# A four-layer fp32 trunk: where ScalarE and VectorE make the parts of the first FFN's down weights

## The chip, the cores and the metric

The kernel runs on one core of one Trainium2 chip. The metric is device time in microseconds (us) of one execution of the whole program. TensorE (PE) multiplies matrices into PSUM banks, ScalarE (ACT) and VectorE (DVE) work element by element, GpSimd (POOL) does some small work and issues loads that add to what is there, and SyncE (SP) issues most of the loads from HBM. Each engine works through its own queue in order; semaphores tie the queues together.

## The reference

The program is a trunk of four layers on one sequence of 512 tokens and 1024 channels, all in fp32. Each layer is a mixer and an FFN with a norm ahead of each; the mixers are a diagonal state-space scan (S5) in layers 0 and 3, gated linear attention (GLA) in layer 1, and differential attention in layer 2. The change is in the first FFN, which computes

```
def rmsnorm(x, g):
    y = xf * lax.rsqrt(jnp.mean(xf * xf, axis=-1, keepdims=True) + NORM_EPS)
    return (y * g)

def swiglu_ffn(h, w_gate_up, w_down):
    g, u = jnp.split(h @ w_gate_up, 2, axis=-1)
    return (jax.nn.silu(g) * u) @ w_down

x = x + swiglu_ffn(rmsnorm(x, norm_ffn[layer]), ffn_w_gate_up[layer], ffn_w_down[layer])
```

with a hidden width of 2816, so `w_down` is 2816 x 1024.

## The kernel before

**Parts.** TensorE works on fp32r operands. To keep fp32 accuracy, each operand is split in two parts: the high part is a cast on ScalarE (`high`, line 348), the low part is the fp32 value minus the high part, on VectorE (`low`, line 356). Three matmuls (`mm3`, lines 376 to 378) then stand for one product: high by high, high by low, low by high.

**Weight tiles.** A weight tile of 128 x 1024 values (512 KB) is loaded by SP into one of three staging buffers (`wst`, line 337, `staged`), cast into one of five part buffers (`whl`), and subtracted. A staging buffer is free for the next load when its subtraction has been done; a part buffer when the last matmul on it is done. For the down weights, one such tile is a pair of k tiles (2 x 128 rows) by 512 output columns (`wb`).

**The FFN.** The hidden width is cut into 11 blocks of 256. For each block the gate and up columns come from seven products of quarter size instead of eight (`seven_block`; `seven_product`, line 543); its named steps run in a fixed order for the first two blocks and in program order for the rest. The last step of a block is `four` and `four_out`: VectorE scales the gate by the row norms (`scaled`, line 588, tile `g`), ScalarE applies silu (line 589), VectorE multiplies it by the other half (line 670), and ScalarE and VectorE make the activation's two parts (lines 680 and 681, tile `act`). In the first FFN (l = 0) the blocks are taken in groups of 3, 3, 3 and 2. After each group comes its down product (`gemm_b`): for each half `d` of the 1024 output columns, over the group's pairs of k tiles `kb`, two k tiles `a`, and four row tiles `t`, one `mm3` into one of four accumulators (`acc`). When the last k tile of an accumulator is done, VectorE adds it to x (line 526). The four accumulator banks are the ones that the gate products `a` and `c` use as well.

**Jobs.** The first and second FFN carry other work with them: after each `mm3`, `gemm_b` calls `self.job()`, which traces the next piece of a generator. In the first FFN this is `s5_spilled`, which prepares the matrices of the last layer's scan in eight rounds and spills them to HBM: small VectorE products (lines 1052 to 1054), ScalarE copies (lines 1119, 1142, 1262), small matmuls (`cps` line 1098, `xps` line 1200, `rps` line 1154) through two shared PSUM banks, and loads and stores on POOL. A job is tied behind the last high part, low part, gate scaling, silu and matmul that were traced before it:

```
    def job(self):
        with ExitStack() as c:
            for y in self.last.values():
                c.enter_context(self.tc.issue_after(y.ins))
            return next(self.jobs, None)
```

**What sets the order.** In this part the order in each engine's queue is made by the planner of the language from priorities and its own estimate of times; `issue_after(ins)` adds an edge by which the instructions traced under it stand behind `ins` in the queue of that engine. `self.last` keeps the latest `scaled` (gate scaling on VectorE) and `silu` (ScalarE). When `self.behind` is set, `high` is tied behind that silu and `low` behind that scaling. `gemm_b` sets `self.behind` from its argument in each step of `kb`, after the first pair's parts have been made, and with jobs it makes the parts of the next pair one step ahead (`nxt`). In the kernel before, the argument is given for the first column half in the FFNs 1 to 3 and is None in FFN 0.

Of the kernel before, what the change touches and what calls it, by code (L numbers as in the profile page):

```python
# [152 lines left out]
class Sides(Left):  # L153
# [19 lines left out]
    def ahead(self, n):  # L173

        w = [self.tr.staged(self.quarter(0, 0, b), 4, 256) for b in range(len(self.heads), len(self.heads) + n)]
        self.heads += [self.tr.halves(y, 4, 256) for y in w]
# [92 lines left out]
class Trunk:  # L269
# [107 lines left out]
        mm(out, lh, rl, start=False, stop=False)  # L377
        self.last["mm"] = mm(out, ll, rh, start=False, stop=last)  # L378

    def gemm_b(self, stat, w, nk, c0, evac, k0=0, tail=0, between=(), ahead=None, jobs=False, behind=None):  # L380

        between = iter(between)
        accs = [self.acc() for _ in range(NT)]
        hl = nxt = None
        for kb in range(0, nk - tail, 2):
            hl = nxt or self.wb(w, k0 + kb, c0)
            self.behind = behind
            nxt = self.wb(w, k0 + kb + 2, c0) if jobs and kb + 2 < nk - tail else None  # L390
            if kb == 2:
                self.flush()
            for a in range(2):
                k = kb + a
                for t in range(NT):
                    self.mm3(
                        accs[t][:], stat(k, 0, t), stat(k, 1, t), hl[:, 0, a], hl[:, 1, a],
                        k == 0, k == nk - 1,
                    )
                    if k == nk - 1:  # L400
                        evac(t, accs[t])
                    if jobs:
                        self.job()
            next(between, lambda: None)()
        self.behind = None
        if tail:
            hls = [self.wb(w, k0 + kb, c0) for kb in range(nk - tail, nk, 2)]
            if ahead:
                self.hand_all()
                ahead()  # L410
            for t in range(NT):
                for j in range(tail):
                    k = nk - tail + j
                    self.mm3(
                        accs[t][:], stat(k, 0, t), stat(k, 1, t), hls[j // 2][:, 0, j % 2],
                        hls[j // 2][:, 1, j % 2], k == 0, k == nk - 1,
                    )
                evac(t, accs[t])
# [270 lines left out]
    def ffn(self, l, left, after=None, turn=False, aside=None, small=None):  # L689


        jobs = bool(aside or small)
# [4 lines left out]
        with self.tc.tile_pool(name=f"ffn{l}", bufs=1, reuse_waits="tile") as fp:  # L697
# [40 lines left out]
            for step in plan.split():  # L738
# [3 lines left out]
                elif name[-1] in "ab":  # L742
                    word = next(w for w in ("split", "add", "high", "low") if name.startswith(w))
                    w = name[len(word) : -1]
# [22 lines left out]
            for nb in (4, 4, 3) if na == 4 else (3, 3, 3, 2):  # L767
                acts = []
                for n in range(b0, b0 + nb):
                    b = blocks[n]  # L770
                    if n > 1:
                        for w in ("direct", "room1", "room22", "room21", "summed"):
                            b[w]()
                    if n > 1:
                        for step in ("one", "one_out", "five", "five_out"):
                            b[step]()
                        b["add"]("22")
                        for step in ("six", "six_out", "two", "two_out", "gate1", "seven", "seven_out", "three", "three_out"):
                            b[step]()
                        b["add"]("21")  # L780
                        b["four"]()
                    acts.append(b["four_out"]())
                stat = lambda k, part, t: acts[k // 2][:, part, k % 2, t * P : (t + 1) * P]
                if b0 + nb == 11 and after is not None:
                    nxt = (Chunks if turn else Left)(self, after)
                for d in range(2):
                    tail = 4 if d == 1 and b0 + nb == 11 else 0
                    self.gemm_b(stat, wd, 2 * nb, d * 512, self.add_x(d, nxt, r), k0=2 * b0, tail=tail, jobs=jobs,
                                behind=None if d or l == 0 else dict(self.last))
                b0 += nb  # L790
            for _ in self.jobs:
                pass
# [1642 lines left out]
```

## Time and profile before

| what | us |
|---|---|
| median of 3 runs | 2316.88 |
| range of these runs | 2314.95 to 2317.75 |
| the profiled execution, own time | 2316.13 |
| its span, first to last instruction | 2314.4 |
| TensorE busy in the span | 2219.4 (96%) |
| VectorE busy | 1593.2 (69%) |
| ScalarE busy | 1108.2 (48%) |
| GpSimd busy | 284.6 (12%) |

The first FFN's four down products start at 301.0, 405.2, 504.7 and 583.8 us of the span. In rows of the profile, a group reads "line engine operation out<-in", with the time that the engine was idle just before it and what ended that wait; a timeline row starts with the start and the length in us. PEld is TensorE's loading of weights, which overlaps its matmuls. A matmul of 128 x 512 is listed with about 0.39 us, but such matmuls follow each other at about 0.227 us, since they are pipelined.

### The profile page before, as it was taken

The page shows a single profiled execution, that of the slowest core. Times are in us where ns is not written, and L with a number is a line of the kernel's source. Part 1 is how long each engine was busy: PE and PEld are TensorE (multiplying, and loading weights), DVE is VectorE, ACT ScalarE, POOL GpSimd, SP SyncE. Part 2 cuts the span into 40 slices and gives each one's busy share as a digit, 9 for nine tenths or more (in the row PEclk, how much of TensorE's full clock was granted, in tenths as well). Part 3 has the DMA queues.
Part 4 walks back from the last instruction along what each step waited for, and adds up shares of the span by engine and source line. Part 5 has one row for each costly group of instructions (what it writes and reads, how often), then busy time and mean ns, then how long its engine had stood idle before and what let it go on. Part 6 is the DMA issues. An engine that isn't in the chain of part 4 may idle for free. (4 is left out here: it accounts for less than half of the span.)

```text
span 2314.4 us, 37179 instructions
## 1 busy us (share of the span) xinstructions
PE 2219.4 (96%) x14847; PEld 1970.1 (85%) x14847; DVE 1593.2 (69%) x2461; ACT 1108.2 (48%) x1769; POOL 284.6 (12%) x394
## 2 busy tenths in 40 slices
PE   5899999999999999999999999999999899999997
PEld 3788979898877799898988787899999788989996
DVE  8784977786624578777745675976766965957674
ACT  5533645454453355555535675654534224635342
POOL 1000140522000010100002131110000100101000
PEclk9999999999999999999999999999999899999999
DMA  4156567663422457665237365886641555766521
GB/s 86 39 146 172 131 173 183 164 179 100 124 71 73 137 140 190 170 177 164 92 124 156 90 152 136 223 210 146 163 103 46 140 153 150 201 157 162 159 80 64
DMA packets 293927, 319.91 MB, mean 138 GB/s; under 512 B 70077, under 2 KB 233177, under 8 KB 293498
## 3 DMA queue, kind: packets, MB, share of 16 engines
q1 hardware_dynamic: 231130, 235.79, 33.6%
q0 software_dynamic: 62624, 81.75, 18.9%
q8 instruction: 117, 1.92, 0.3%
q14 instruction: 56, 0.46, 0.1%
HBM read 285.62 MB, written 16.65 MB: 131 GB/s over the span
## 5 line engine op out<-in xcount | busy, mean ns | idle before, releaser
L356 DVE TENSOR_TENSOR whl<-wst,whl 128x1024 fp32r<-128x1024 f32 x272 | 331.1, 1222 | 264.5 <-ACT whl L348 263.4
L348 ACT CAST whl<-wst 128x1024 fp32r<-128x1024 f32 x272 | 284.3, 1050 | 336.9 <-PE acc L378 232.8
L543 PE MATMUL a<-side,whl 128*128 128x256 f32 x3168 | 382.4, 277 | 6.1 <-DVE whl L356 6.0
L543 PEld LDWEIGHTS a<-side,whl 128*128 128x128 f32 x3168 | 369.9, 188 | 7.8 <-DVE whl L356 6.7
L376 PE MATMUL acc<-whl,act 128*128 128x512 f32 x704 | 278.0, 395 | 2.6 <-DVE g L588 2.6
L377 PE MATMUL acc<-whl,act 128*128 128x512 f32 x704 | 274.9, 390 | 0.0
L378 PE MATMUL acc<-whl,act 128*128 128x512 f32 x704 | 274.7, 390 | 0.0
L543 PE MATMUL c<-side,whl 128*128 128x256 f32 x2112 | 256.2, 278 | 7.2 <-DVE whl L356 7.2
L543 PEld LDWEIGHTS c<-side,whl 128*128 128x128 f32 x2112 | 248.4, 189 | 8.2 <-DVE whl L356 8.2
L356 DVE TENSOR_TENSOR whl<-slot,whl 128x1024 fp32r<-128x1024 f32 x105 | 127.8, 1222 | 66.0 <-ACT whl L348 65.9
L376 PEld LDWEIGHTS acc<-whl,act 128*128 128x128 f32 x704 | 132.1, 188 | 31.9 <-DVE g L588 3.0
L378 PEld LDWEIGHTS acc<-whl,act 128*128 128x128 f32 x704 | 132.2, 188 | 27.9
L377 PEld LDWEIGHTS acc<-whl,act 128*128 128x128 f32 x704 | 132.2, 188 | 25.9 <-issue 0.2
L348 ACT CAST whl<-slot 128x1024 fp32r<-128x1024 f32 x105 | 110.0, 1053 | 74.0 <-PE acc L378 28.2
L376 PE MATMUL acc<-whl,hT 128*128 128x512 f32 x352 | 142.8, 406 | 2.1 <-DVE ro L2160 1.5
L377 PE MATMUL acc<-whl,hT 128*128 128x512 f32 x352 | 138.0, 392 | 0.9 <-DVE whl L356 0.9
L378 PE MATMUL acc<-whl,hT 128*128 128x512 f32 x352 | 138.1, 392 | 0.0
L543 PE MATMUL a<-sides,whl 128*128 128x256 f32 x1056 | 133.9, 283 | 1.2 <-DVE x L526 1.2
L543 PE MATMUL d<-sides,whl 128*128 128x256 f32 x1056 | 133.4, 282 | 1.3 <-ACT whl L348 1.3
L543 PEld LDWEIGHTS a<-sides,whl 128*128 128x128 f32 x1056 | 129.4, 191 | 2.3 <-issue 1.6
L543 PEld LDWEIGHTS d<-sides,whl 128*128 128x128 f32 x1056 | 128.8, 191 | 1.9 <-ACT whl L348 1.9
L680 ACT CAST act<-r 128x512 fp32r<-128x512 f32 (+1 forms) x110 | 66.2, 644 | 105.1 <-DVE r L661 86.1
(449 smaller groups left out, 3901.1 us busy)
## 6 DMA issues: line engine op xcount, KB each, us to landing
wst<-in_ffn_w_gate_up_dram SPq DMA_DIRECT2D x88, 512.0 KB, 4.5
wst<-in_ffn_w_down_dram SPq DMA_DIRECT2D x88, 512.0 KB, 4.4
slot<-in_ffn_w_gate_up_dram SPq DMA_DIRECT2D x69, 512.0 KB, 5.8
wst<-in_ffn_w_gate_up_dram POOLq DMA_DIRECT2D x44, 512.0 KB, 6.1
halves<-in_ffn_w_gate_up_dram SPq DMA_DIRECT2D x42, 512.0 KB, 5.5
wst<-in_s_w_glu_dram SPq DMA_DIRECT2D x32, 512.0 KB, 4.9
wst<-in_gla_w_in_dram SPq DMA_DIRECT2D x24, 512.0 KB, 3.6
wst<-in_diff_w_qkv_dram SPq DMA_DIRECT2D x24, 512.0 KB, 4.0
```

What stands on the lines that cost most here:

```text
L348: self.last["high"] = self.nc.scalar.copy(hl[:, 0], w[:])
L356: self.last["low"] = self.nc.vector.tensor_tensor(hl[:, 1], w[:], hl[:, 0].bitcast(F32), op=ALU.subtract)
L376: mm(out, lh, rh, start=first, stop=False)
L377: mm(out, lh, rl, start=False, stop=False)
L378: self.last["mm"] = mm(out, ll, rh, start=False, stop=last)
L543: mm(o, hl[:, x, k, c], side[:, y, k], start=first and not (j or k or n), stop=k == 3 and n == 2, skip_group_check=True,)
L680: self.last["act high"] = nc.scalar.copy(dst[:, 0, j], src[:, j])
```

## The change

`gemm_b` gets an argument `few`, and `self.behind` is set from the argument `behind` only in steps with `kb < few`. The call in `ffn` gives `behind` for the first column half in all four FFNs, with `few=2` in FFN 0 and `few=2 * nb` (every step) in the others. As a pair's parts are made one step ahead in FFN 0, the step `kb = 0` makes the second pair under the rule, and from `kb = 2` on the rule is off; the first pair is made before the rule is set.

```diff
-    def gemm_b(self, stat, w, nk, c0, evac, k0=0, tail=0, between=(), ahead=None, jobs=False, behind=None):
+    def gemm_b(self, stat, w, nk, c0, evac, k0=0, tail=0, between=(), ahead=None, jobs=False, behind=None, few=0):
...
             hl = nxt or self.wb(w, k0 + kb, c0)
-            self.behind = behind
+            self.behind = behind if kb < few else None
             nxt = self.wb(w, k0 + kb + 2, c0) if jobs and kb + 2 < nk - tail else None
...
                     self.gemm_b(stat, wd, 2 * nb, d * 512, self.add_x(d, nxt, r), k0=2 * b0, tail=tail, jobs=jobs,
-                                behind=None if d or l == 0 else dict(self.last))
+                                behind=None if d else dict(self.last), few=2 if l == 0 else 2 * nb)
```

In the order that is built, ScalarE has five casts of down tiles ahead of the activation's last cast in each of the first three groups of FFN 0 before, of which four stand behind the first pair's; after the change only the first pair's cast stands ahead of the last silu, the second pair's stands between the silu and the activation's last cast, and the others follow. VectorE's subtractions move in the same way. The scan's jobs stand in other places among them. On TensorE the big matmuls keep their order and some groups of the jobs' small matmuls move by a few places. POOL's spills and accumulating loads change places among themselves, and on SP one load of the next layer moves behind four small ones. From the next layer's start on, the queues are as before.

## The prediction

> **What bounds the kernel now.** I read the page from the top, busy shares first, then the waits of TensorE alone in the first FFN, then the timelines of VectorE and ScalarE around each wait.
>
> ```profile
> span 2314.4 us, 37179 instructions
> PE 2219.4 (96%) x14847; PEld 1970.1 (85%) x14847; DVE 1593.2 (69%) x2461; ACT 1108.2 (48%) x1769; POOL 284.6 (12%) x394
> ```
>
> TensorE is busy for 96% of the span; the kernel is as long as its matmul stream plus the holes in it. An edit that takes no matmul away can win only holes. So the question is how many holes lie in the stretch that the change touches, the first FFN (about 250 to 609 us). The waits of TensorE from 290 to 640 us are these two, and from 317.2 to 630 us the same view lists none:
>
> ```profile
> PE acc L376 <- DVE g L588: 2.6, 1, 2.6
> PE xps L1200 <- DVE halves L1054: 1.3, 1, 1.3
> ```
>
> Both lie in the first of the four down products of this FFN. The next view sets the first three down products side by side (columns: stretch, length, busy time and count of PE, PEld, DVE, ACT, POOL, granted clock, DMA share, GB/s); the fourth row is the last down product, the fifth the first one of the second FFN, where the parts already stand behind the gate.
>
> ```profile
> 301.00:346.98 45.98, 41.94 (x298) 31.15 (x296) 33.90 (x80) 18.60 (x47) 24.15 (x38) 1.00 0.60 156
> 405.17:446.61 41.44, 41.44 (x298) 31.27 (x297) 32.38 (x77) 17.19 (x45) 28.22 (x48) 1.00 0.53 141
> 504.69:545.03 40.34, 40.34 (x290) 30.68 (x289) 27.38 (x59) 16.14 (x39) 23.69 (x40) 1.00 0.55 138
> 583.76:608.87 25.11, 25.11 (x127) 20.67 (x125) 19.42 (x29) 13.37 (x27) 0.13 (x1) 1.00 0.30 86
> 911.59:955.00 43.41, 43.41 (x194) 35.69 (x193) 33.97 (x109) 25.89 (x45) 3.55 (x5) 1.00 0.49 148
> ```
>
> The first two hold the same 298 matmuls, and the first is 45.98 − 41.44 = 4.54 us longer, of which 45.98 − 41.94 = 4.04 us is idle. Products two to four have no idle time at all. Hence a ceiling: about 4.0 us, at the very most 4.5, of 2314 (0.17 to 0.2%).
>
> Where the 4.04 us come from is seen in the timelines of TensorE, ScalarE and VectorE at the first down product (start, length, instruction, idle before it and its cause):
>
> ```profile
> 298.28 2.88 PE L543 MATMUL a<-side,whl 128*128 128x256 f32 x24
> 303.64 0.40 PE L378 MATMUL acc<-whl,act 128*128 128x512 f32 x1
> 306.59 0.51 PE L376 MATMUL acc<-whl,act 128*128 128x512 f32 x1 [2.56 <-DVE g L588]
> 312.99 0.68 PE L1200 MATMUL xps<-ident,halves 64*64 64x64 f32 x16 [1.33 <-DVE halves L1054]
> 316.46 0.39 PE L376 MATMUL acc<-whl,act 128*128 128x512 f32 x1
> 316.99 0.27 PE L1154 MATMUL rps<-halves 128*32 128x64 f32 x2
> 300.34 0.69 DVE L661 TENSOR_TENSOR r<-r,r 128x512 f32<-128x512 f32 x1
> 303.63 1.05 ACT L348 CAST whl<-wst 128x1024 fp32r<-128x1024 f32 x1 [5.18 <-DMA wst<-in_ffn_w_down_dram]
> 304.71 1.23 DVE L356 TENSOR_TENSOR whl<-wst,whl 128x1024 fp32r<-128x1024 f32 x1 [3.68 <-ACT whl L348]
> 305.86 0.68 DVE L588 TENSOR_TENSOR g<-a,R 128x512 f32<-128x512 f32 x1
> ```
>
> The down product's fourth accumulator takes the bank that the gate's last scaling (L588, g) still has to read. That scaling was ready when the last gate product ended, 298.28 + 2.88 or about 301.2, but stood in VectorE's queue behind the subtraction of a later down tile (L356 at 304.71), which waited for its ScalarE cast, which waited for a load until 303.63. TensorE stood for 2.56 us. The spilled scan's first transposes (xps) then came 1.33 us late, because their VectorE work had been pushed back with the rest; 0.15 us more is lost ahead of 316.99.
>
> **The change, part by part.** It adds and removes no matmul, cast, subtraction or load; it changes places in the queues. In the code only the pair of down tiles made at the first step (the second pair, k tiles 2 and 3) is bound to stand behind the last gate's scaling and silu; the first pair is made before the rule is set. But tiles of one pool and queue follow each other, so in the built order all later pairs of this product, and those of its second half, fall behind as well: ScalarE had five casts ahead of the last silu or its activation cast and now has one, VectorE likewise. This holds at all four down products of the first FFN. The other FFNs' orders are unchanged.
>
> *Gate scaling forward.* At the first product L588 can start at 301.2 to 301.3, since the activation's subtraction before it (0.68) only needs L661, over at 301.0. The bank is free at 302.0, TensorE wants it at 304.0 (303.64 plus one step). The 2.56 us go, fully on the path. Cost of the cover: none, nothing else asks for that bank.
>
> *Second pair later.* What it costs the second pair is shown by the second FFN, which has this order now (first five rows; the last three are the first FFN's):
>
> ```profile
> 911.85 0.68 DVE L588 TENSOR_TENSOR g<-a,R 128x512 f32<-128x512 f32 x1
> 912.63 0.63 ACT L589 ACTIVATE g<-g 128x512 f32<-128x512 f32 x1 [1.42 <-DVE g L588]
> 913.17 1.03 ACT L348 CAST whl<-wst 128x1024 fp32r<-128x1024 f32 x1
> 914.23 1.23 DVE L356 TENSOR_TENSOR whl<-wst,whl 128x1024 fp32r<-128x1024 f32 x1 [0.25 <-ACT whl L348]
> 915.49 13.71 SPq L337 DMA_DIRECT2D wst<-in_ffn_w_down_dram  x4
> 294.96 5.14 SPq L337 DMA_DIRECT2D wst<-in_ffn_w_down_dram  x3
> 310.29 0.17 DVE L1133 MEMSET halves<- 64x128 f32 x1
> 311.13 0.22 DVE L1054 TENSOR_TENSOR halves<-halves 128x64 f32<-128x64 f32 x1
> ```
>
> Parts ready 914.23 + 1.23 − 911.59 = 3.9 us after the product starts; TensorE reaches that pair after 24 matmuls (about 0.227 us each from 303.64 to 316.46, 5.5 us) plus the small ones between, 6 to 7 us. Covered by 2 us or more at each product, in the fourth by 1.6. Zero. If that cover went, each us late would be a us of idle.
>
> *Staging buffers later.* This is what the edit really costs. There are three staging buffers; each is refilled only when its subtraction is done, as the load at 915.49 shows, right behind the subtraction. Before, SP could issue the down loads at 294.96 and the two next behind it (a run of three, ended by 300.10); now the first of these keeps its time, the second goes out at about 304.9 and the third behind the third pair's subtraction, which ends about 6.7 us into the product (3.9, the second activation subtraction 0.7, the scan's first VectorE operations 1.0, as from 310.29 to the end of 311.13, and 1.2 for itself), so at 307.8 in the first; in the second, without the two memsets, 6.4 us in, at 411.6. ScalarE's order then puts the cast of that last tile ahead of the four scan copies L1119, and VectorE's Q operations (two L1052, L1053, L1054) wait for them; TensorE's rps matmuls wait for those. So a load is now in the chain to TensorE, where none was.
>
> How long is a load? The views of the DMA queues, in the stretches 294.9 to 300, 305.9 to 309, 405 to 409 and 915 to 919 us, say (median us from issue to landing):
>
> ```profile
> wst<-in_ffn_w_down_dram SPq DMA_DIRECT2D x3, 512.0 KB, 8.6
> wst<-in_ffn_w_gate_up_dram SPq DMA_DIRECT2D x2, 512.0 KB, 3.5
> wst<-in_ffn_w_gate_up_dram SPq DMA_DIRECT2D x2, 512.0 KB, 4.5
> wst<-in_ffn_w_down_dram SPq DMA_DIRECT2D x2, 512.0 KB, 4.0
> ```
>
> The bounds are 3.5 and 8.6. The 8.6 belongs to a crowd: three down loads, gate loads and an accumulating load within 8 us. The new order spreads them, some 2 to 3 us apart, as in the last two rows; I take 4.4. From landing to the rps matmuls:
>
> ```profile
> 413.50 0.94 ACT L1119 ACTIVATE halves<-cps 64x64 f32<-64x64 f32 x4
> 413.63 1.23 DVE L356 TENSOR_TENSOR whl<-wst,whl 128x1024 fp32r<-128x1024 f32 x1 [0.87 <-ACT whl L348]
> 414.77 0.42 DVE L1052 TENSOR_TENSOR halves<-halves,pw 128x256 f32<-128x256 f32 x1
> 415.78 0.42 DVE L1054 TENSOR_TENSOR halves<-halves 128x256 f32<-128x256 f32 x1
> 419.37 0.45 PE L1154 MATMUL rps<-halves 128*32 128x64 f32 x16
> 521.51 0.45 PE L1154 MATMUL rps<-halves 128*32 128x64 f32 x16
> 592.82 1.43 DVE L526 SCALAR_TENSOR_TENSOR x<-acc,rcol,x 128x512 f32<-128x512 f32 x2 [1.05 <-PE acc L378]
> ```
>
> A cast of 1.05, then the subtraction (1.2) beside the copies (0.94), then 1.43 from 414.77 to the end of L1054: 3.7 us; in the first product the subtraction stands behind those operations, so about 3.2.
> - First product: landed 307.8 + 4.4 = 312.2, Q ready 315.4. TensorE without its old holes reaches rps at about 314.5 (31 matmuls from 303.06, 0.7 for xps, 15 more). Wait 0.9. Ahead of it xps is ready at about 310.35, TensorE there at 310.3: 0.1. Later small groups there are regrouped, 0.2 by estimate. Together 1.2.
> - Second: landed 416.0, Q ready 419.7 against 419.37: 0.3.
> - Third: rps comes at the 61st matmul instead of the 52nd; ready 504.7 + 6.4 + 4.4 + 3.7 = 519.2, reached 521.5. Zero; 0.1 for a copy out of a shared bank that may be tight.
> - Fourth: no scan work. The next layer's first casts and subtractions move behind the x additions on VectorE (L526, from 592.82), 1.2 us each, in front of the h products that TensorE transposes. I find about 0.3 us of room at the tightest, and count zero.
>
> *Moved past.* On SP one GLA load goes behind four small ones, and the gate tiles of the next blocks are issued 2 to 4 us later. The next gate product starts only at 346.98, over 30 us behind these issues, so zero. On POOL the accumulating loads and the scan's spills change places; the accumulated tiles too are for that next gate stage, so zero again.
>
> Sum: −(2.56 + 1.33 + 0.15) + 1.2 + 0.3 + 0.1 = −2.4 us. The profiled execution took 2316.13 (span 2314.4); the sum puts its like at 2313.7. The median of the three runs stands 0.75 higher, so 2314.5.
>
> The Trainium skill, page "DMA: Bandwidth & Descriptors", section "Anatomy of one DMA — SWDGE (gpsimd) path", gives a fit of about 2.0 us plus bytes over 436 GB/s, for another issuing path; for 512 KB that is an estimate of 3.2 us, and by it the new waits would shrink to about 0.8 and the time to 2313.7. The trace does not reach it: its shortest is 3.5.
>
> **Rivals.**
> *All hidden.* The loads land in 3.5 or so and the regrouping costs nothing; only the ceiling counts: 2316.9 − 4.0 to 4.5 = 2312.4 to 2312.9. For it: products two to four had no hole. Against it: in the new order a load feeds the scan's chain.
> *The load becomes the wait (slower).* If landing takes 8.6, as at 294.96, first product 1.2 + 4.2 = 5.4, second 4.5, third 1.9 (8.6 − 4.4 less the 2.3 of room): 11.8 against 4.04, +7.8, so 2324.7. The turning point is 1.6 + 2 (L − 4.4) = 4.04, L = 5.6; slower by over 0.2% needs about 7.3. Against it: the crowd is thinned by the very change. Idle of that length also drew the clock down in this trace:
>
> ```profile
> 1502.96 1.44 PE L543 MATMUL c<-side,whl 128*128 128x256 f32 x7 [4.30 <-DVE whl L356]
> 1503.00:1506.00 3.00, 3.00 (x16) 3.00 (x17) 2.09 (x3) 0.87 (x1) 0.00 (x0) 0.58 1.17 239
> ```
>
> That is 3 × 0.42 = 1.3 us more for each such wait, 2327 with two. The Trainium skill's page "TensorE: Matmul & The Clock Gate", Part 1, names about 3.4 us of idle as enough for half clock; by this row the trace agrees, and the 2.56 us hole (clock 1.00) is short of it.
> *The change does not do what it says.* It binds the second pair alone, and the scan's operations take over the hole: xps stays at 312.99 because the casts ahead of it on ScalarE wait. Then 2316 to 2317. Against it: the tile whose load held everything until 303.63 keeps its issue time and is needed only at 308.
>
> **How the numbers follow.** 0.2% is 4.6 us here, about what a measurement of this kernel can tell from no change. My sum 0.55; all hidden 0.17 (0.13 of it beyond 0.2%, as the ceiling lies just at it); load becomes the wait 0.22 (0.20 beyond); no effect 0.06. Faster 0.13, same 0.67, slower 0.20. The range 2312.0 to 2320.5 takes in the ceiling and landing times up to about 6.7; it leaves out some 0.05 below and 0.14 above.
>
> **What would show it.** In the new trace: L588 (g) of the first down product within 0.4 us of its first matmul; no wait of L376 on L588; the down loads of the first product in two late steps near 305 and 308, landing in 4 to 5 us; a wait of rps (L1154) on VectorE L1054 or of TensorE behind L1119 of under 1 us in products one and two; product one about 43 us, the others within 0.5 of 41.4, 40.3 and 25.1. A landing over 5.6 us, or an idle rps of several us in product two or three, would prove me wrong.

## The result, and the profile after

| what | before | after |
|---|---|---|
| median of 8 runs each | 2317.11 us | 2324.01 us |
| range of these runs | 2314.76 to 2319.80 | 2318.79 to 2327.34 |
| the profiled execution, own time | 2316.13 | 2326.70 |

The ratio after to before is 1.0028, with a 95% interval of 1.0017 to 1.0038: 4 to 9 us slower. The forecast, 2314.5 with a range of 2312.0 to 2320.5, was wrong in sign and missed with its range.

The head of the page of the changed kernel:

```profile
span 2325.0 us, 37177 instructions
PE 2229.9 (96%) x14847; PEld 1978.1 (85%) x14847; DVE 1592.2 (68%) x2461; ACT 1107.2 (48%) x1769; POOL 284.9 (12%) x394
```

The same matmuls, and TensorE is busy for 10.5 us more, almost the whole difference of the spans (10.6). The same matmuls were busy for longer, so much of this difference need not lie in the waits. The two profiles, set side by side instruction by instruction, part in three places. By the first product's first matmul (305.17 against 301.00) after is 4.17 us behind, although no instruction ahead of that product's last gate block differs. From there to the end of the fourth down product it loses 4.19 us more. About 60 us behind that, in the GLA layer, it loses another 1.6.

The first and the third are clock. The stretch of the start, before and then after (columns as in the prediction: length, busy time and count of PE, PEld, DVE, ACT, POOL, granted clock, DMA share, GB/s):

```profile
40.00:140.00 100.00, 89.02 (x813) 75.14 (x809) 85.80 (x142) 54.35 (x91) 7.27 (x19) 0.90 0.24 49
```

```profile
40.00:140.00 100.00, 89.35 (x755) 74.31 (x750) 81.67 (x135) 53.31 (x89) 7.19 (x18) 0.85 0.22 48
```

0.90 against 0.85 over 100 us is 5 us of clock. Whether that belongs to the change is settled below by profiling before again. What the change can have done lies in the down products. Those of the changed kernel:

```profile
305.17:352.75 47.58, 42.97 (x285) 32.53 (x283) 34.25 (x79) 20.03 (x48) 23.31 (x37) 0.96 0.59 149
411.50:454.45 42.95, 41.71 (x299) 31.40 (x297) 35.16 (x79) 19.91 (x48) 27.84 (x48) 1.00 0.57 157
512.53:552.99 40.46, 40.44 (x290) 30.68 (x289) 30.01 (x61) 18.84 (x42) 22.99 (x39) 1.00 0.63 159
591.73:617.23 25.50, 25.38 (x127) 20.51 (x125) 21.27 (x30) 14.86 (x29) 0.13 (x1) 1.00 0.32 83
```

Against 45.98, 41.44, 40.34 and 25.11 these are +1.60, +1.51, +0.12 and +0.39; 14 small matmuls that left the first product for the gate stage behind it add 0.56. The waits of TensorE there:

```profile
PE xps L1200 <- DVE halves L1054: 4.1, 1, 4.1
PE rps L1154 <- DVE halves L1052: 1.2, 1, 1.2
PE rps L1154 <- DVE halves L1054: 0.5, 1, 0.5
```

The wait of L376 on L588 is gone, and a longer one has come in its place, at the scan's transposes (xps). Where it comes from is read backwards in the timelines of TensorE, VectorE and POOL:

```profile
305.44 0.68 DVE L588 TENSOR_TENSOR g<-a,R 128x512 f32<-128x512 f32 x1
321.39 1.31 POOL L579 DMA_DIRECT2D wst<-in_ffn_w_gate_up_dram  x1 [2.83 <-ACT halves L1262]
322.74 1.46 POOL L1302 DMA_DIRECT2D out<-halves  x1
331.44 0.36 DVE L1053 TENSOR_TENSOR halves<-halves,pw 128x192 f32<-128x192 f32 x1 [4.13 <-DMA out<-halves]
332.85 0.35 DVE L1054 TENSOR_TENSOR halves<-halves 128x192 f32<-128x192 f32 x1
333.35 1.12 PE L1200 MATMUL xps<-ident,halves 64*64 64x64 f32 x16 [4.11 <-DVE halves L1054]
```

VectorE cannot begin the next round of Q (L1053 at 331.44), because the last round's Q is still being spilled (L1302, `out`): there is one Q buffer. The spill went out at 322.74, 1.35 us behind an accumulating load of a gate tile (L579). The views of the DMA queues around 322 us, after and then before (median us to landing):

```profile
wst<-in_ffn_w_gate_up_dram POOLq DMA_DIRECT2D x1, 512.0 KB, 8.4
out<-halves POOLq DMA_DIRECT2D x1, 256.0 KB, 8.7
```

```profile
wst<-in_ffn_w_gate_up_dram POOLq DMA_DIRECT2D x1, 512.0 KB, 7.3
out<-halves POOLq DMA_DIRECT2D x1, 256.0 KB, 3.7
```

Before, that accumulating load had gone out at 313.11, 5.1 us ahead of the spill, and the spill landed in 3.7 us. Counted from the product's begin, the spill goes out only 0.4 us later in after, but the accumulating load 4.1 us. By the order of the program its base tile is the second gate tile that SP loads in this product: that one went out at 316.10 instead of 308.37, 3.6 us later from the begin, since the down tiles' subtractions freed the staging buffers later. The bracket of the load's row names ACT L1262, which ended last (321.02); but the longest of POOL's own waits at this line is the one for that tile, 2.94 us until it had landed at 320.77 (the row gives the shortest, median and longest wait in ns):

```profile
L579 POOLq EVENT_SEMAPHORE  x5: 17/43/2938, 317.8 to 330.7; - x5
```

Behind the hole the clock fell (the hole with the xps matmuls, then the 14 big matmuls after it):

```profile
328.85:334.40 5.55, 1.44 (x18) 0.96 (x17) 2.96 (x5) 0.00 (x0) 2.73 (x5) 0.88 0.40 111
334.40:338.46 4.06, 4.06 (x15) 3.30 (x14) 3.63 (x13) 1.64 (x7) 2.67 (x6) 0.74 0.84 143
```

0.12 x 5.55 + 0.26 x 4.06 = 1.7 us. So the 4.19 us come out as 1.9 more of holes (5.97 against 4.04 over the four products), 1.7 of clock and about 0.5 left over. That rest lies in the busy times of products two and four (41.71 and 25.38 us against 41.44 and 25.11); I put it down to small matmuls that stand in other places, which no run tests.

In the second product ScalarE shows the wait that I had forecast, the scan's copies behind a cast that waits for its load:

```profile
423.22 1.05 ACT L348 CAST whl<-wst 128x1024 fp32r<-128x1024 f32 x1 [2.72 <-DMA wst<-in_ffn_w_down_dram]
424.18 0.94 ACT L1119 ACTIVATE halves<-cps 64x64 f32<-64x64 f32 x4
```

That load was issued at 417.82, so it took about 5.3 us.

### The profile page after: what moved, and what is told of

It is laid out like the page before. It is cut to its first block, busy times and chain, and to the rows that moved or that the text cites. A ratio compares the mean times of both kernels' runs of the same rounds, so it can differ in the third digit from the quotient of the medians.

```text
span 2325.0 us, 37177 instructions
## 1 busy us (share of the span) xinstructions
PE 2229.9 (96%) x14847; PEld 1978.1 (85%) x14847; DVE 1592.2 (68%) x2461; ACT 1107.2 (48%) x1769; POOL 284.9 (12%) x394
## 5 line engine op out<-in xcount | busy, mean ns | idle before, releaser
L376 PE MATMUL acc<-whl,act 128*128 128x512 f32 x704 | 278.3, 396 | 0.0
L376 PEld LDWEIGHTS acc<-whl,act 128*128 128x128 f32 x704 | 132.4, 188 | 29.2 <-issue 1.2
L376 PE MATMUL acc<-whl,hT 128*128 128x512 f32 x352 | 143.9, 409 | 2.1 <-DVE ro L2160 1.5
```

The costliest lines, as they stand in the source:

```text
L376: mm(out, lh, rh, start=first, stop=False)
```

## The experiments

"Stretch" is the time from the first product's first matmul to the end of the fourth product; in the first profile of before it is 608.87 - 301.00 = 307.87 us. It leaves out the start and the GLA layer. Each row is one profile; the ratio comes from the timed runs (5 to 12 of each changed kernel beside 17 to 29 of before; 8 of each for after).

| kernel | product one | product two | stretch | against 307.87 | ratio to before |
|---|---|---|---|---|---|
| before | 45.98 | 41.44 | 307.87 | | |
| before again | 45.76 | 41.43 | 307.67 | -0.20 | |
| after | 47.58 | 42.95 | 312.06 | +4.19 | 1.0028 [1.0017, 1.0038] |
| after again (first) | 49.78 | 43.24 | 314.40 | +6.53 | |
| after again (second) | 49.29 | 43.73 | 314.33 | +6.46 | |
| product one alone | 49.26 | 41.44 | 311.69 | +3.82 | 1.0033 [1.0020, 1.0045] |
| products two to four alone | 44.87 | 45.42 | 311.45 | +3.58 | 1.0016 [1.0008, 1.0025] |
| after, load held behind the spill | 43.02 | 43.16 | 307.03 | -0.84 | 1.0001 [0.9991, 1.0012] |
| product one alone, load held | 42.99 | 41.44 | 304.88 | -2.99 | 0.9990 [0.9981, 0.9999] |
| load held, copies first | 42.32 | 43.08 | 306.23 | -1.64 | 1.0002 [0.9991, 1.0012] |
| subtraction alone | 44.27 | 42.12 | 306.98 | -0.89 | 0.9997 [0.9988, 1.0005] |
| second half's first pair alone | 42.52 | 41.43 | 304.40 | -3.47 | 0.9990 [0.9981, 0.9999] |
| the same again | 42.21 | 41.44 | 304.11 | -3.76 | 0.9991 [0.9979, 1.0004] |

### The two halves of the change

Product one alone:

```diff
-                                behind=None if d else dict(self.last), few=2 if l == 0 else 2 * nb)
+                                behind=None if d or (l == 0 and b0) else dict(self.last), few=2 if l == 0 else 2 * nb)
```

> The new order at the first of the four down products alone; the other three keep the order of before. Theory A (the loss is made in the places that the trace of after shows: 4.11 us of xps and a lower clock behind it in product one, a late down load in product two): product one with the gate stage behind it comes out 2.2 us longer than before (106.3 against 104.2), with one hole of about 4 us at the second xps group; products two to four as before (41.4, 40.3, 25.1); time +2 us, about 2319. Theory B (most of the loss lies outside the first FFN, in the granted clock of the start, 4.1 us, and behind the FFN, 1.6 us, which fell low by chance in the profiled run): the first FFN is the same as by A, but the median over the runs shows only noise of 1 to 2 us. Theory C (the loss is made by all four products alike): +1.7 us.

Products two to four alone:

```diff
-                                behind=None if d else dict(self.last), few=2 if l == 0 else 2 * nb)
+                                behind=None if d or (l == 0 and not b0) else dict(self.last), few=2 if l == 0 else 2 * nb)
```

> The new order at products two to four, product one as before (its two holes of 2.56 and 1.33 us stay). Theory A: product two 42.9 us with an rps hole of 1.2 us behind a down load that lands 5.3 us after its issue, product three 40.5, product four 25.5; time +2.0 us, about 2319. My prediction's step (rps wait 0.3 in product two, 0.1 in three, none in four) would give +0.4. If e1 and this one add up to less than 5 us over before, the rest of the measured 6.9 us is clock or a consequence of where the later stages begin.

Each costs more than I had read from the profile of after: 3.8 us instead of 2.2, and 3.6 instead of 2.0. With product one alone, that product's row and its long wait are

```profile
303.35:352.61 49.26, 44.34 (x284) 33.46 (x282) 34.38 (x79) 20.03 (x48) 23.22 (x37) 0.93 0.58 143
```

```profile
PE xps L1200 <- DVE halves L1054: 4.4, 1, 4.4
```

With products two to four alone, the rows of products one and two, and then two of the waits, are

```profile
300.45:345.32 44.87, 41.92 (x298) 31.14 (x296) 33.89 (x79) 18.61 (x47) 24.14 (x38) 1.00 0.64 162
403.53:448.95 45.42, 43.12 (x298) 32.35 (x297) 35.33 (x79) 19.90 (x48) 27.29 (x47) 0.96 0.56 148
```

```profile
PE rps L1154 <- DVE halves L1052: 2.3, 1, 2.3
...
PE acc L376 <- DVE g L588: 1.0, 1, 1.0
```

The holes are in the places that theory A names, so A holds for the places, though not for the sizes. The surplus is a longer hole in product two (2.3 against 1.2) and clock: 0.93 in product one against 0.96, and 0.96 in product two against 1.00. Theory B falls, since each half is slower than before in the timed runs too, clear of 1; theory C falls, since products three and four account for 0.7 of the 3.6. The timed runs of product one alone (4.6 to 10.4 us) lie above its one stretch; five runs don't settle that. The row of product one in the second kernel also shows that before's own hole is not fixed: the wait on L588, 2.56 us in the first profile, is 1.0 here under the same order.

### Is it the load ahead of the spill?

```diff
-            if plus:
-                nc.gpsimd.dma_start(w[:], left.quarter(*plus, b), accum_op=ALU.add)
+            with self.tc.issue_after(self.outs[0].ins) if name == "3" and b == 3 and len(getattr(self, "outs", ())) in range(1, 8) else nullcontext():
+                plus and nc.gpsimd.dma_start(w[:], left.quarter(*plus, b), accum_op=ALU.add)
```

`self.outs` lists the spills L1302 as they are traced; the condition picks one tile, in the first FFN. Everything else is as in after.

> The changed kernel with one accumulating gate load (the one that POOL issued at 321.39 ahead of the first spill) held behind that spill. Theory A1 (the spill landed late, 8.7 us after its issue instead of 3.7, because it stands behind that load on POOL's queue): the spill lands in 3 to 5 us, the hole of 4.11 us ahead of the second xps group falls to under 1 us, the clock stays at 1.00 in product one, product one with the gate stage behind it about 102.5 us; time about 4 us under that of the changed kernel. Theory A2 (the whole DMA is crowded there, whatever the order on POOL): the spill still takes 7 us or more and the hole stays over 2.5 us; time as the changed kernel's.

The spill in the view of the DMA queues, the rows of products two and one, and the wait of xps with this edit:

```profile
out<-halves POOLq DMA_DIRECT2D x1, 256.0 KB, 5.6
```

```profile
402.55:445.71 43.16, 41.71 (x298) 31.41 (x297) 35.14 (x79) 19.88 (x48) 27.48 (x47) 1.00 0.59 156
301.33:344.35 43.02, 41.77 (x299) 31.48 (x297) 35.08 (x81) 20.08 (x48) 23.25 (x37) 1.00 0.60 153
```

```profile
PE xps L1200 <- DVE halves L1054: 0.3, 1, 0.3
```

The hole of 4.11 us is 0.34, the clock in product one is 1.00, and the time is back at that of before. A1 holds, though the spill takes 5.6 us, a little over my 3 to 5: something else, perhaps the gate loads of SP beside it, slows it as well. How far the accumulating load goes out ahead of the spill, and how long the spill then takes, over the profiles: 5.1 us ahead, 3.7 (before); 3.3, 4.6 (subtraction alone); 3.0, 4.1 (second half's first pair); 1.35, 8.7, and 1.34 with 9.1, 9.1 and 9.7 (the four profiles with the new order in product one). Counted from the load's landing, though, the spill is alike in all of them: in all ten profiles in which the load goes out first, the spill lands 0.9 to 1.6 us behind it, in before too (load at 320.36, spill at 321.93). So the spill stands behind the load in any case, and the distance only tells how much of the load is still to come. In after the load goes out 4.1 us later and takes 8.4 us instead of 7.3, and so the spill lands 5.3 us later in the product.

A count over all thirteen profiles, between 250 and 640 us, speaks for the order of POOL's queue and against a crowd on the whole DMA (A2): of the 389 transfers that POOL issued while an accumulating load was under way, none landed ahead of that load; of SP's, 61 of 218 did. The Trainium skill, page "DMA: Bandwidth & Descriptors", section "Two DMAs through the same engine are not ordered", says that within one queue of one DMA engine descriptors start in order but are pipelined, so that an earlier one need not have finished writing when a later one completes. The trace agrees with the order and shows no later one that landed first.

With the load held, the change at product one alone:

> The new order at product one alone, with the accumulating gate load held behind the first spill: the change at the one place where before has holes, without the step that my prediction had put at zero. Theory A (the spill behind that load is the whole of the loss in product one, the rest of the predicted sum holds): product one 42.5 to 43.5 us, one rps wait of about 0.5 us, product two 41.4 again; the stretch from the first product's first matmul to the end of the fourth product about 2.5 to 3 us shorter than before; time 2314 to 2315, near that of the run in which only the second half's first pair was bound. Rival (the earlier scaling of the gate is worth nothing here, since another wait takes each hole): the stretch as long as before, time 2317.

Products one and two:

```profile
302.09:345.08 42.99, 41.76 (x298) 31.46 (x297) 35.17 (x81) 20.07 (x48) 23.26 (x37) 1.00 0.60 153
403.27:444.71 41.44, 41.44 (x298) 31.27 (x297) 32.29 (x77) 17.14 (x45) 28.28 (x48) 1.00 0.56 141
```

For the first product that is what my prediction had: -2.99 us in the stretch, where the sum had -2.8 for this product, and 0.999 of before. All of the first product's loss is in the step that the held load takes out. With the new order at all four products and the load held, the stretch is only 0.84 us shorter than before, against 2.4 in the sum; what is missing there is mostly product two (43.16 against 41.44).

### The second product's wait

On top of the held load:

```diff
-            self.behind = behind if kb < few else None
+            self.behind = behind if kb < few else dict(silu=self.cps[27], scaled=self.cps[27]) if late and kb + 4 == nk else None
```

(`cps[27]` is the last of the four copies L1119 in product two; `late` is set for the second half of that product.)

> The changed kernel with the accumulating load held behind the first spill, and in product two the cast of the last down pair put behind the four scan copies (L1119) that stood behind it on ScalarE; the load itself stays as late. Theory A (rps of product two waits because those copies stand behind a cast whose load lands 5.3 us after its issue): the rps wait in product two falls from 1.2 to 2.3 us to under 0.3, product two about 41.5. Rival (the scan's own small loads, which land late as well there, 422.95 in the changed kernel, are what VectorE waits for): the wait stays over 1 us. Time by A 2316 to 2317.5, by the rival 2318.5.

The row of product two, and the waits of the first FFN's down products:

```profile
405.62:448.70 43.08, 42.02 (x298) 31.29 (x297) 35.02 (x79) 19.99 (x48) 27.51 (x47) 1.00 0.59 155
```

```profile
PE rps L1154 <- DVE halves L1054: 1.0, 2, 0.5
PE acc L376 <- DVE x L526: 0.6, 1, 0.6
```

Half right. The rps wait of product two falls from 1.45 us with the held load alone to 0.50, so the cast in front of the copies does carry it. But the product is no shorter (43.08 against 43.16): VectorE now waits 0.57 and 0.69 us for the scan's small loads ahead of its Q operations, and 0.56 us come back at an accumulator whose bank waits for an addition to x (L526). One late chain, moved, shows the next.

### Half of the binding

```diff
-        with self.tc.issue_after(self.behind["silu"].ins) if self.behind else nullcontext():
+        with self.tc.issue_after(self.behind["silu"].ins) if self.behind and self.behind.get("cast", True) else nullcontext():
...
-                                behind=None if d else dict(self.last), few=2 if l == 0 else 2 * nb)
+                                behind=None if d else dict(self.last, cast=l > 0), few=2 if l == 0 else 2 * nb)
```

> The changed kernel with half of its binding in the first FFN: only the second pair's subtraction on VectorE is put behind the gate's scaling; its cast on ScalarE stays free, as before. Theory A (the cost comes from the late casts, which delay the subtractions, the staging buffers and so the gate loads behind them): the casts and the loads keep their times, only one subtraction slides behind the scaling, the 2.56 us hole goes and no long wait comes; product one 42 to 43.5 us, product two 41.4; time 2313.5 to 2315.5. Rival (the late subtraction alone frees the buffer late, and the casts do not matter): the last down loads of product one go out 8 us later as in the changed kernel, with a hole of over 1 us in product one or two; time 2317 or more.

The timeline of VectorE at the first product, and two of TensorE's waits:

```profile
306.57 1.23 DVE L356 TENSOR_TENSOR whl<-wst,whl 128x1024 fp32r<-128x1024 f32 x1 [2.85 <-ACT whl L348]
307.71 0.69 DVE L588 TENSOR_TENSOR g<-a,R 128x512 f32<-128x512 f32 x1
```

```profile
PE xps L1200 <- DVE halves L1054: 1.4, 1, 1.4
PE acc L376 <- DVE g L588: 1.1, 1, 1.1
```

Neither theory. With the casts free only one subtraction slides behind the scaling, and another still stands ahead of it, waiting for its load. So the gate's scaling is not first, and the hole shrinks to 1.1 us. The loads did not keep their times either: counted from the product's begin, the last two down loads went out 2.4 and 4.8 us later than before. In sum -0.9 us in the stretch, a time that can't be told from before. The subtraction that has to stand behind the scaling is the one that waits for its load, and in the change it is the bound casts that bring this about, with the late buffers that come with it.

### The pair that matters, alone

On the kernel before, only the pair whose load landed at 303.53 is bound:

```diff
-        hl = nxt = None
+        hl = nxt = None; self.behind = first
...
-                stat = lambda k, part, t: acts[k // 2][:, part, k % 2, t * P : (t + 1) * P]
+                stat = lambda k, part, t: acts[k // 2][:, part, k % 2, t * P : (t + 1) * P]; gate = dict(self.last)
...
-                                behind=None if d or l == 0 else dict(self.last))
+                                behind=None if d or l == 0 else dict(self.last), first=gate if d and l == 0 and not b0 else None)
```

> Another binding, on the kernel before: only the first pair of the second half of product one (the one whose load lands at 303.53 and whose subtraction stood ahead of the gate's scaling) is put behind the last gate's scaling and silu; no other pair, and no other product. The loads keep their order and their buffers are freed at most 0.7 us later. Theory A: the 2.56 us hole goes and nothing takes its place, because the two pairs ahead are split as early as before; product one 42 to 43.4 us, the rest as before; time 2.5 to 4 us under before, 2313 to 2314.5. If putting the gate ahead brings a new wait whatever is bound (the rival), product one stays at 45 us or more and the time at 2316 or more.

> The version in which only the first pair of product one's second half stands behind the gate, measured again: by its trace the first FFN is 3.5 us shorter than in the first profile of before; ratio to before 0.998 to 0.9995, product one 42 to 43 us with at most 1.2 us of holes and no granted clock under 1 in it. A ratio of 1.000 or above would mean that the first measurement's gain was chance.

Product one in its first profile:

```profile
301.73:344.25 42.52, 41.41 (x299) 31.13 (x297) 33.93 (x79) 18.78 (x47) 24.62 (x39) 1.00 0.69 174
```

The holes there are 0.8 and 0.3 us; in the second profile 0.4 and 0.4. The stretch is 3.5 and 3.8 us shorter than before, so by the traces theory A holds. The timed runs give 0.9990 [0.9981, 0.9999] and 0.9991 [0.9979, 1.0004]: two medians about 2 and 3 us under before (2.5 to 4 were expected), one interval clear of 1 and one that just touches it. By the ratios this version is about 9 us faster than the changed kernel; over before its gain is at the edge of what these runs can tell.

### Before and after, profiled again

> The kernel before, unchanged, profiled once more. It has the same instructions as the changed one up to the first FFN. If the granted clock of the start is a matter of chance, the begin of the first FFN (255 us) lies anywhere from 1.3 us earlier to 4.1 us later than in the first profile of before, as it did in the six profiles so far; the rows of the first product (2.56 and 1.33 us of waits, no granted clock under 1) come out within 1.5 us of the first profile's.

Its first product, and its only wait there that the view lists:

```profile
303.76:349.52 45.76, 43.48 (x298) 32.31 (x296) 33.96 (x80) 18.60 (x47) 24.14 (x38) 0.96 0.62 154
```

```profile
PE acc L376 <- DVE g L588: 2.2, 1, 2.2
```

The expectation on the start holds: the same kernel reaches the first product 2.76 us later than in its first profile, and over all thirteen profiles, whose orders are one up to the last gate block ahead of that point, the begin lies between 300.45 and 305.83 us. The 4.17 us of the first comparison are chance. The expectation on the clock fell: with a shorter hole (2.20 instead of 2.56, and no xps wait) the product is as long, because the granted clock is 0.96.

The GLA layer is chance too. The same 32 us there, first before, then before again, after, and after again (each from its own profile):

```profile
668.00:700.00 32.00, 32.00 (x154) 26.41 (x153) 9.52 (x12) 6.00 (x8) 0.00 (x0) 0.95 0.26 80
```

```profile
668.00:700.00 32.00, 32.00 (x145) 26.87 (x144) 8.69 (x9) 7.52 (x10) 0.00 (x0) 0.89 0.30 84
```

```profile
668.00:700.00 32.00, 32.00 (x137) 25.54 (x136) 8.43 (x8) 12.15 (x17) 0.00 (x0) 0.89 0.28 85
```

```profile
668.00:700.00 32.00, 32.00 (x145) 25.49 (x144) 10.34 (x11) 12.15 (x17) 0.00 (x0) 0.95 0.34 99
```

Both values occur in both kernels.

> The changed kernel once more. In its first profile the stretch from the begin of the first FFN's last gate products to the end of the fourth down product was 4.2 us longer than before, while the medians differ by 6.9; the two halves of the change run apart gave 3.8 and 3.5, together 7.4, because a hole sometimes brings a stretch of granted clock near 0.5 behind it (1.2 to 2.6 us more) and sometimes none. Theory A (the rest of the 6.9 is such clock stretches behind the new holes, which fall differently in each execution): the long xps hole (4 to 4.5 us) and the rps hole of product two (1.2 to 2.3 us) come again, and the stretch is 4 to 7.5 us longer than before. Theory B (the rest is the start and the stage behind the FFN, which the change does not touch): the stretch comes out at 4.2 again, within 0.5.

> As the run ahead of it, a third profile of the changed kernel, to see the spread: by theory A 4 to 7.5 us over before in the first FFN, by theory B 4.2 within 0.5.

Product one in the first of these two, and its waits:

```profile
302.28:352.06 49.78, 44.11 (x285) 33.30 (x283) 34.18 (x79) 20.05 (x48) 23.26 (x37) 0.93 0.59 143
```

```profile
PE xps L1200 <- DVE halves L1054: 4.9, 1, 4.9
PE rps L1154 <- DVE halves L1052: 1.5, 1, 1.5
PE rps L1154 <- DVE halves L1054: 0.8, 1, 0.8
```

Theory A: the stretch is 6.5 us over before in both, whose single times, 2323.92 and 2327.03, lie 6.2 and 9.3 us over that session's median of before (2317.71). The three profiles of after give 4.2, 6.5 and 6.5, 5.7 on average, the two of before 0.0 and -0.2. A loss of 5.8 us in the first FFN lies inside the interval of the medians (4 to 9) and accounts for most of their 6.9; the rest is not settled and need not be anything but chance.

## Why the prediction was wrong

- *Gate scaling forward.* Right. L588 runs 0.27 us after the product's first matmul, and the wait of L376 on it is gone in every profile with the bound casts. With no long wait in its place it is worth 3.0 to 3.8 us (-2.99, -3.47, -3.76), under the ceiling of 4.0 to 4.5.
- *Second pair later, covered.* Right: no wait of an accumulating matmul on that pair's parts in the waits of any profile.
- *Staging buffers later.* The chain was right in place and hour. Counted from the product's begin, the last two down loads of product one were forecast 3.9 and 6.8 us in and went out 3.8 and 6.6 us in, landing in 4.7 and 3.6 us (I took 4.4); in product two the last one was forecast 6.4 us in and went out 6.3 us in. In product one the rps wait was 0.5 us (0.8 and 1.1 in the repeats) against 0.9. In product two it was mis-sized: 1.2, 1.5 and 2.0 us, and 2.3 in the run of products two to four, against 0.3, because the load took 5.3, 5.6, 6.1 and 6.4 us there instead of 4.4. Each of these waits is its load's time less 4.1 us, as it was in the sum (4.4 less 0.3), so the chain was right and the load's time wrong.
- *Third and fourth product.* +0.1 as said, and +0.4 instead of zero, of which 0.12 is a wait.
- *Moved past: the step that failed.* "On POOL the accumulating loads and the scan's spills change places; the accumulated tiles too are for that next gate stage, so zero again." I asked only who needs the accumulated tile, not who needs the transfer behind it. The gate tiles went out 2 to 4 us later, as written, and that was enough to send the accumulating load out 4.1 us later, 1.35 us ahead of a spill that lands only behind it. The spill's buffer is what VectorE's next round writes into. That step measured 4.1 to 4.9 us of hole instead of zero, and holding the one load behind the spill took it out (0.3).
- *The clock.* I had it as a side remark under a rival, 1.3 us for each wait of 4.3 us, and took the hole of 2.56 us as too short for it; the profile of before again shows a loss behind 2.20 us. Behind the xps hole it cost 1.7 us in the first profile and about 3 in the repeats (busy time 44.1 in product one, with 0.56 more for the matmuls that left it, against 41.8 with the hole closed).
- *The ceiling.* 4.0 to 4.5 us was read from one profile, in which the hole of 2.56 us cost no clock. In the second profile of before the holes are 2.3 us and clock takes 1.5 (busy 43.48 against 41.94). The ceiling was about right, its make-up a matter of chance.
- *The rivals.* "The load becomes the wait" gave 2324.7, and 2324.0 was measured, but not by its mechanism: the two late down loads of product one took 4.7 and 3.6 us in the changed kernel's first profile, the one of product two 5.3, all under the turning point of 5.6, and only in product two of the repeats did a load reach it (5.6 and 6.1, for a wait of 1.5 and 2.0 us). Most of the loss came by another transfer, on another queue, so the agreement of the two numbers is luck. "The change does not do what it says" is refuted by L588. The chance of 0.20 for slower was too low, since the transfers that I had put at zero had no bounds in the range.
- *Side sums.* Two are off and change nothing in the forecast: with a load of 3.2 us the new waits of the sum come to 0.4 us and the time to about 2313.2, not to 0.8 and 2313.7, and being slower by 0.2% takes a landing of about 7.5 us by the terms of the sum, not 7.3. The shortest load of 512 KB by SP in the first profile took 3.36 us, not 3.5.

## What to carry to other kernels

When an edit moves a load, follow the transfers that stand behind it in its queue as well as the load's own reader: the buffer that a late store still holds can stop an engine that has nothing to do with the load. To bring one instruction forward, bind only what stands waiting in front of it, here one pair out of six, and leave the producers that free buffers where they are. And price a hole on TensorE with the clock behind it: at the same place a hole of 2.56 us cost its own length in one execution, and one of 2.20 us cost about 1.5 us on top in the next.

## What the runs showed of the hardware

- The granted clock falls to half for stretches of 3.41 us, so in portions of 1.7 us lost, and whether a hole brings one is partly chance: no portion behind 2.56 us of idle (before), behind 1.2, 1.5 and 2.0 (product two of after's three profiles), behind 1.0 and 1.8 (products two to four alone, product one) or behind 1.1 and 1.4 (subtraction alone); one behind 2.20 us (before again) and behind 2.30 (products two to four alone, product two); one or two behind 4.1 to 4.9. In before again the 3.41 us ahead of the slow stretch, and the slow stretch itself, are

```profile
306.89:310.30 3.41, 1.31 (x6) 1.09 (x7) 3.06 (x4) 2.28 (x4) 0.22 (x1) 1.00 0.64 211
310.30:313.71 3.41, 3.41 (x10) 2.67 (x9) 2.63 (x9) 0.62 (x1) 0.00 (x0) 0.50 0.78 248
```

  The Trainium skill, page "TensorE: Matmul & The Clock Gate", section "What's actually happening", tells of a free-running window of about 3.4 us, after one idle one of which the clock is halved. The trace agrees with the portions (half of 3.4 is 1.7) and with the chance, but not with a wholly idle window as the condition, since 2.20 us were enough, with TensorE busy for 1.31 us of such a window.
- A TensorE that counts as busy can lose its clock as well: the GLA layer's 32 matmuls of 128x2 (`dps`), which take 3.6 to 4.1 us in the first profiles of before and after, were followed by one or two such stretches in each of the thirteen profiles (0.95 or 0.89 over 32 us in the four shown). The traces show the order of events, not the reason.
- On POOL's queue a store of 256 KB that was issued while an accumulating load of 512 KB was under way landed behind that load, 0.8 to 2.5 us later, in all 37 such cases of the thirteen profiles between 250 and 640 us; the other 57 stores took 3.0 to 5.6 us.
- The same instructions of the start took from 300.45 to 305.83 us to the first down product over thirteen profiles, a spread of 5.4 us; the timed runs of before spread by 11 to 13 us in each session.
